# Low weight halves of the first steps on VectorE alone, the first result split behind them; one of the last turned row tiles ahead of the last products, rows sent whole

## The chip, the cores and the metric

The kernel runs on one core of a Trainium2 chip. The time is the device time of one execution in microseconds (us), and the figure used is the median of the runs. Engines are TensorE (PE in the profile, its weight loads PEld), VectorE (DVE), ScalarE (ACT), GpSimd (POOL) and SyncE (SP). An engine's instruction queue bears a small q (SPq).

## The reference

One decoder layer is computed for 512 prompt tokens and for 8 x 4 sample tokens together, 544 rows of width 1024, all in fp32:

```python
def _layer(x, ...):
    m, ... = _mixer(_rmsnorm(x, norm_mix_pre), ...)
    x = x + _rmsnorm(m, norm_mix_post)
    f, ... = _conv_ffn(_rmsnorm(x, norm_ffn_pre), ...)
    return x + _rmsnorm(f, norm_ffn_post)

def _mixer(h, ...):
    xr, q, k, v, g = split(h @ w_in)            # 1024 -> 1024 | 1024 | 256 | 256 | 2048
    lru_out = _rg_lru(_causal_dwconv(xr, ...))
    attn = _band_attention(q, k, v, d, valid, sink, rel_bias)     # window 128, 8 heads on 2
    ...
    merged = sigmoid(g_lru) * (lru_out @ w_lru_o) + sigmoid(g_attn) * (attn @ w_attn_o)
    return merged @ w_out

def _conv_ffn(h, prev, w_up, conv_w, conv_b, w_down):
    u = _causal_dwconv(h @ w_up, ...)           # 1024 -> 8192, width 3
    val, gate = split(u)
    return (gelu(gate) * val) @ w_down          # 4096 -> 1024
```

The scores of the attention get a bias that depends on the distance of query and key, looked up in a table of 32 buckets (`rel_bias`). The states of the recurrences, the last keys and values and the last rows before each convolution are outputs too.

## The kernel before

**How a product is made.** A matrix product in fp32 is three products of split operands: each number is a high half and a low half, and TensorE adds high x high, high x low and low x high into one bank (`mmhalf`). The high half of a weight is a rounded copy by ScalarE (`wsplit_hi`, L275, `wh_in<-raw_in`), and the low half is what is left, raw minus high, by VectorE or GpSimd (`wsplit_lo`, L280, `wl_in<-raw_in,wh_in`). Activations stand turned, features on partitions and tokens along the free side, in two halves of 256 and 288 tokens. `h` is the normalized input, `hH` and `hL` its halves (`hsplit`, L431 and L175).

**The order of the work.** Nearly all instructions stand on their engines in the order in which the program writes them, and semaphores hold an engine until its operands are there. A `step` multiplies one chunk of 128 output columns with one half of the tokens (24 matmuls into a bank `pm...`) and then calls `tick`. A `tick` hands out, in this order: high halves of the next weight units (ScalarE), whatever runs beside (`sides`: the normalization of the second token half, tables, attention), what the step before wanted done with its result (the list `late`), the low halves, and what was put in the list `last`. A weight unit is half a chunk's weights, 128 x 512; a step asks for two of them. Before the change the second low half of a step goes to GpSimd as long as the clock of steps, `now`, is at most 6, and all others go to VectorE.

**The head.** The chunks of the input projection come as two keys and value chunks and the first queries. The first step's bank is `pm_first`; it is filled piece by piece as the turned pieces of `h` come. Its result is a key, whose halves are made by ScalarE (`kH`, L651) and VectorE (`kL`, L166, `kL<-pm_first,kH`). Meanwhile the second token half is normalized: squares of `x` by ScalarE and VectorE (`jv<-x`, L407), the root and its correction (L389, L175), the scaling of the rows (L423), the turning by TensorE (`ps_tb`, L508) and the split into `hH` and `hL`; copies of `x` itself (`xn<-ps_ta`, L483) free the banks that the last turns take. On GpSimd's queue a chain for the bias table runs: `rvec` is written to DRAM (`rscr`), read back spread over the distances (`rrep`, L627) and once more into `btab` (L633). VectorE adds `btab` to the first scores (`s<-psc,btab`, L175); after maxima and the exponential, TensorE turns the weights of the attention (`pt`, L753).

**The tail.** The result of the down projection leaves in rows of tokens. The prompt's first two tiles of 128 tokens are multiplied with tokens on the output's partitions (`ptok`, and for the last 512 columns of tile 1 two pieces of 256, `pend`, made by `ends`), normalized there (`ssq`, the root at L1862, a reciprocal and its correction) and added to `x` (`xtok<-fg,nst_t,xtok`, `tokens_out`), 512 columns at a time. Tiles 2 and 3 and the 32 sample tokens (tile 4) are normalized while still turned (`finish_b`, tiles `ft`), and `rows_t` turns them back: four transposes into a bank `pyo` for each half of 512 columns, a copy by ScalarE into `yo` and a transfer on SP's queue. The function `ends` makes 12 matmuls and two transposing ones for each piece, and both pieces stand ahead of all of `rows_t` on TensorE. The list that sets SP's order at the end is

```python
    yo = [rows_t(i, kk) for i in (2, 3, 4) for kk in range(2)]
    ...
    for f in yo[:3] + xo[:1] + yo[3:4] + xo[1:] + yo[4:]:
        f()
```

Of the kernel before, what the change touches and what calls it, by code (L numbers as in the profile page):

```python
# [17 lines left out]
P = 128  # L18
# [103 lines left out]
def hawk_step(ctx, tc, I, O):  # L122
# [69 lines left out]
    def tick(target=0, dt=1):  # L192
        now[0] += dt
        todo = late[:]
        late.clear()
        split = [wsplit_hi(u) for u in wclaim(target)]
        sides()
        for f in todo:
            f()
        for z, u in enumerate(split):  # L200
            wsplit_lo(*u, eng=pool if z and now[0] <= 6 else None)
        for f in last:
            f()
        last.clear()
# [117 lines left out]
    def step(key, X, a, done, target=None, look=2, quick=False):  # L322

        first_ = key == order[0] and a == 0
        ps = first_ps if first_ else PM("pm" + "_".join(str(z) for z in key) + f"_{a}")
        if first_:
            pass
        elif quick:
            mmhalf(ps, key, X, a, range(4))
            now[0] += 0.5  # L330
            sides()
            mmhalf(ps, key, X, a, range(4, 8))
            done(a, ps)
        else:
            mmhalf(ps, key, X, a)
        tick(upto(key, a, look) if target is None else target, 0.5 if quick else 1)
        if not quick:
            late.append(lambda: done(a, ps))


    xp = I["x_prompt"][0]
# [1385 lines left out]
            if c % 2:  # L1727
                yield 0.5

    def rows_t(i, kk):  # L1730
        t0, nn, _ = TOK[i]
        dst = yp[t0:t0 + nn, :] if i < 4 else ys
        px = PX(f"pyo{i}_{kk}")
        for j in range(4):
            pe.transpose(px[:nn, j * P:(j + 1) * P], ft[4 * kk + j][:, t0:t0 + nn], ident)
        o = S(f"yo{i}_{kk}")[:nn, 0:512]
        act.copy(o, px[:nn, :])
        return lambda: nc.sync.dma_start(out=dst[:, kk * 512:(kk + 1) * 512], in_=o)

    sq7 = T("sq7")  # L1740
    frow, fgs = {}, {}
# [110 lines left out]
    fgs[1, 1] = T("fg1_1")[:, 0:512]  # L1852
    st = SM("nst_t1", [P, 4], "nst_t")
    v, r, s_, b_ = (st[:, z:z + 1] for z in range(4))
    o = ends(0)
    ends_square(0, o)
    ends_gain(0, o)
# [3 lines left out]
    ends_square(1, o)  # L1861
    act.activation(s_, ssq[:, 1, 2:3], AF.Sqrt, scale=1.0 / D, bias=b_)  # L1862
    ends_gain(1, o)
    yo = [rows_t(i, kk) for i in (2, 3, 4) for kk in range(2)]
    stt(v, ssq[:, 1, 2:3], 1.0 / D, b_, ALU.mult, ALU.add)
    dve.reciprocal(r, s_)
    mul(s_, r, r)
    stt(s_, s_, -0.5, v, ALU.mult, ALU.mult)
    stt(r, s_, 1.5, r, ALU.add, ALU.mult)
    xo = [tokens_out(1, r, z) for z in range(2)]  # L1870
    for f in yo[:3] + xo[:1] + yo[3:4] + xo[1:] + yo[4:]:
        f()
    flush()
    order_.close()
# [32 lines left out]
```

## Time and profile before

| | before |
|---|---|
| median of 3 runs, us | 1001.16 (1001.01 to 1002.63) |
| the profiled execution, us | 1000.28 |
| its span, us | 998.3 |
| granted TensorE clock over the span | 0.997 |
| TensorE busy, us | 987.0 |
| VectorE, ScalarE, GpSimd busy, us | 731.4, 580.0, 171.9 |
| moved by DMA | 135.90 MB, mean 136 GB/s |

By stretches of the span, from the busy times of the engines in each:

| stretch, us | length | TensorE busy | VectorE busy | ScalarE busy | GpSimd busy | clock | DMA share |
|---|---|---|---|---|---|---|---|
| 0 to 50 (load, first projections) | 50.0 | 45.97 | 27.87 | 32.05 | 12.82 | 0.97 | 0.70 |
| 50 to 245 | 195.0 | 195.00 | 127.69 | 106.51 | 29.57 | 1.00 | 0.38 |
| 245 to 440 | 195.0 | 195.00 | 124.11 | 107.60 | 68.21 | 1.00 | 0.36 |
| 440 to 600 | 160.0 | 159.61 | 129.98 | 104.13 | 13.45 | 1.00 | 0.57 |
| 600 to 900 | 300.0 | 300.00 | 250.01 | 176.35 | 31.50 | 1.00 | 0.71 |
| 900 to 970 | 70.0 | 69.46 | 55.93 | 45.55 | 6.00 | 1.00 | 0.55 |
| 970 to 998.3 (tail) | 28.3 | 21.98 | 15.81 | 7.78 | 10.31 | 0.95 | 0.22 |

A row of the engines' lists begins with the start time from the span's beginning and the length, both in us, and then has the engine, the line of the program, the operation, what it writes and reads, and the tile's shape. A row that stands for several instructions has their count at its end (x12), and its length reaches from the first's start to the last's end. Square brackets hold the time in which the engine stood idle just before it and what it waited for. The clock is the share of full speed that the chip granted TensorE.

### The profile page before, as it was taken

Reading aid. Unit: us, or ns where it says so; the run is one execution under the profiler, and the core shown is the slowest. Engines: PE = TensorE matmul, PEld = TensorE weight load, DVE = VectorE, ACT = ScalarE, POOL = GpSimd, SP = SyncE. Lnnn points to the kernel's source line nnn. Section 1 sums busy time; section 2 is a strip of 40 time slices with the busy share of each in tenths; the row PEclk is TensorE's granted clock in tenths of the full one; section 3 lists DMA queues with packets and bytes.
Section 4 is the critical chain, followed back from the end, with each engine's and each line's share of the span. In section 5 each row is a group of like instructions: output and inputs, shape, how many; then the busy total and the mean of one; then the engine's idle time right before and its main releaser. Section 6 shows DMA issues by size and latency. Waiting matters only on the chain.

```text
span 998.3 us, 20177 instructions
## 1 busy us (share of the span) xinstructions
PE 987.0 (99%) x7811; PEld 976.8 (98%) x7811; DVE 731.4 (73%) x1533; ACT 580.0 (58%) x1417; POOL 171.9 (17%) x281
## 2 busy tenths in 40 slices
PE   8999999999999999999999999999999999999997
PEld 7999999999999999999999999999999999999996
DVE  6466688545936656589777788888888888888765
ACT  7534455469458625456776656565656565656652
POOL 2252010001404473210001011111110101011004
PEclk9999999999999999999999999999999999999999
DMA  7656323332323635226156767676767676768612
GB/s 209 183 133 214 102 64 106 106 85 81 110 69 100 191 92 144 85 88 206 55 117 140 178 135 184 137 181 140 178 142 175 144 174 147 171 143 206 196 45 90
DMA packets 212118, 135.90 MB, mean 136 GB/s; under 512 B 9549, under 2 KB 197725, under 8 KB 211992
## 3 DMA queue, kind: packets, MB, share of 16 engines
q1 hardware_dynamic: 200056, 113.00, 39.6%
q0 software_dynamic: 11920, 19.59, 12.0%
q10 hardware_dynamic: 48, 2.03, 0.8%
q8 instruction: 61, 1.00, 0.4%
q14 instruction: 33, 0.27, 0.1%
HBM read 112.06 MB, written 11.37 MB: 124 GB/s over the span
## 4 chain that ended last, share of the span: by engine, by line
PE 93%; DVE 2%; ACT 1%; SPq 1%; DMA 1%; issue 0%; ACTq 0%; DVEq 0%
PE pmin L163 21%; PE pmdn L163 17%; PE pux L1458 16%; PE puy L1458 8%; PE pq L1458 6%; PE pmout L163 5%; PE pmao L163 5%; PE pmlo L163 5%; PE puz L1458 4%; PE pg L163 1%; PE psc L163 1%; PE pvp L163 1%; DMA x<-in_x_prompt_dram 1%; SPq L354 1%; PE pt L753 1%; PE ptok L163 1%
## 5 line engine op out<-in xcount | busy, mean ns | idle before, releaser
L163 PE MATMUL pmin<-hH,wh_in 128*128 128x256 f32 (+1 forms) x568 | 166.6, 293 | 0.3 <-ACT wh_in L275 0.3
L163 PE MATMUL pmin<-hH,wl_in 128*128 128x256 f32 (+1 forms) x568 | 164.0, 289 | 1.9 <-DVE wl_in L280 1.9
L163 PE MATMUL pmin<-hL,wh_in 128*128 128x256 f32 (+1 forms) x568 | 164.3, 289 | 0.0
L163 PE MATMUL pmdn<-fH,wh_dn 128*128 128x256 f32 (+1 forms) x448 | 129.4, 289 | 0.2 <-DVE ft L172 0.2
L163 PE MATMUL pmdn<-fH,wl_dn 128*128 128x256 f32 (+1 forms) x448 | 129.0, 288 | 0.0
L163 PE MATMUL pmdn<-fL,wh_dn 128*128 128x256 f32 (+1 forms) x448 | 129.0, 288 | 0.0
L175 DVE SCALAR_TENSOR_TENSOR uc<-u,fv,uc 128x560 f32<-128x560 f32 x128 | 102.1, 798 | 13.3 <-ACT uc L1489 13.2
L163 PEld LDWEIGHTS pmin<-hH,wh_in 128*128 128x128 f32 x568 | 107.9, 190 | 1.9 <-issue 1.2
L163 PEld LDWEIGHTS pmin<-hH,wl_in 128*128 128x128 f32 x568 | 107.6, 189 | 2.1 <-DVE wl_in L280 2.1
L163 PEld LDWEIGHTS pmin<-hL,wh_in 128*128 128x128 f32 x568 | 107.7, 190 | 0.0
L163 PEld LDWEIGHTS pmdn<-fH,wh_dn 128*128 128x128 f32 x448 | 84.4, 188 | 0.6 <-issue 0.6
L163 PEld LDWEIGHTS pmdn<-fH,wl_dn 128*128 128x128 f32 x448 | 84.4, 188 | 0.0
L163 PEld LDWEIGHTS pmdn<-fL,wh_dn 128*128 128x128 f32 x448 | 84.2, 188 | 0.0
L1584 ACT COPY u<-pux 128x272 f32<-128x272 f32 x52 | 20.1, 386 | 84.9 <-PE pux L1458 84.9
L166 DVE TENSOR_TENSOR u<-puy,u 128x240 f32<-128x240 f32 (+2 forms) x78 | 24.7, 344 | 49.3 <-PE puy L1458 32.4
L172 DVE TENSOR_TENSOR ft<-ft,pmdn 128x256 f32<-128x256 f32 (+1 forms) x104 | 45.3, 437 | 17.2 <-PE pmdn L163 16.8
L275 ACT ACTIVATE wh_in<-raw_in 128x512 fp32r<-128x512 f32 x72 | 44.4, 631 | 18.4 <-PE pmin L163 7.1
L1489 ACT ACTIVATE uc<-u,fv 128x560 f32<-128x560 f32 x64 | 48.2, 755 | 0.0
L280 DVE TENSOR_TENSOR wl_in<-raw_in,wh_in 128x512 fp32r<-128x512 f32 x66 | 45.1, 692 | 0.8 <-ACT wh_in L275 0.7
L716 ACT ACTIVATE s<-s,st 128x256 f32<-128x256 f32 (+1 forms) x32 | 15.2, 476 | 48.0 <-DVE st L713 39.6
L1384 POOL DMA_DIRECT2D raw_up_s<-raw_up_s x26 | 22.7, 872 | 100.2 <-DMA raw_up_s<-raw_up__10515 4.5
L166 DVE TENSOR_TENSOR wl_dn<-raw_dn,wh_dn 128x512 fp32r<-128x512 f32 x56 | 38.4, 686 | 0.0
(781 smaller groups left out, 3431.4 us busy)
## 6 DMA issues: line engine op xcount, KB each, us to landing
raw_in<-in_w_in_dram SPq DMA_DIRECT2D x36, 512.0 KB
raw_dn<-in_w_down_dram SPq DMA_DIRECT2D x56, 256.0 KB
raw_up_s<-in_w_up_dram SPq DMA_DIRECT2D x25, 512.0 KB
raw_up_s<-raw_up_s POOLq DMA_DIRECT2D x26, 256.0 KB, 5.9
raw_ao<-in_w_attn_o_dram SPq DMA_DIRECT2D x8, 512.0 KB
raw_lo<-in_w_lru_o_dram SPq DMA_DIRECT2D x8, 512.0 KB
raw_out<-in_w_out_dram SPq DMA_DIRECT2D x8, 512.0 KB
xdram<-xn POOLq DMA_DIRECT2D x8, 272.0 KB, 14.7
```

Of the source, the lines that this page charges most:

```text
L163: pe.matmul(out, l, r, start=start, stop=stop)
L166: dve.tensor_tensor(out=out, in0=a, in1=b, op=ALU.subtract)
L172: dve.tensor_tensor(out=out, in0=a, in1=b, op=ALU.add)
L175: dve.scalar_tensor_tensor(out=out, in0=a, scalar=s_, in1=b, op0=op0, op1=op1)
L275: act.activation(hl[0], raw, AF.Copy)
L280: (eng or dve).tensor_tensor(out=hl[1], in0=raw, in1=f32(hl[0]), op=ALU.subtract)
L354: nc.sync.dma_start(out=xt[i, z][:n, 0:512], in_=src[:, 512 * z:512 * z + 512])
L716: act.activation(s3[:, j, :], s3[:, j, :], AF.Exp, bias=ng[:, j:j + 1], accum_out=sm[:, j:j + 1])
L1384: pool.dma_start(out=w["p4"], in_=w["p2"], accum_op=ALU.add)
L1458: pe.matmul(ps[:, :HN], w, x, start=start and k == 0 and i == 0, stop=stop and k == 3 and i == 2, skip_group_check=True)
L1489: act.activation(yt[j][:, 0:FLATU], u[:, 0:FLATU], AF.Copy, scale=fv[:, j:j + 1])
L1584: act.copy(e[nm_], z)
```

## The change

It has two parts that do not touch each other.

At the head, every low half that a `tick` hands out is made by VectorE, also the second ones of the first ticks that GpSimd made before (the two for the very first step, outside of any tick, stay on GpSimd); and the split of the first step's result (`kH`, `kL`) is put in the list `last` instead of `late`, so that in its tick it comes behind the low halves instead of ahead of them.

At the tail, `rows_t` handles a whole row of 1024 columns: both banks are copied into one tile (from the buffers of the weights, `RAW`), and one transfer takes 1024 columns where two took 512 each. Tile 2 is turned ahead of both pieces of `ends`, tiles 3 and 4 behind them as before. SP's list has the two tiles of prompt rows first, then the first half of the last token-major tile, the sample rows, and its second half.

```diff
--- before.py
+++ after.py
@@ -197,8 +197,8 @@
         sides()
         for f in todo:
             f()
-        for z, u in enumerate(split):
-            wsplit_lo(*u, eng=pool if z and now[0] <= 6 else None)
+        for u in split:
+            wsplit_lo(*u)
         for f in last:
             f()
         last.clear()
@@ -335,7 +335,7 @@
             mmhalf(ps, key, X, a)
         tick(upto(key, a, look) if target is None else target, 0.5 if quick else 1)
         if not quick:
-            late.append(lambda: done(a, ps))
+            (last if first_ else late).append(lambda: done(a, ps))
 
 
     xp = I["x_prompt"][0]
@@ -1727,15 +1727,16 @@
             if c % 2:
                 yield 0.5
 
-    def rows_t(i, kk):
+    def rows_t(i):
         t0, nn, _ = TOK[i]
         dst = yp[t0:t0 + nn, :] if i < 4 else ys
-        px = PX(f"pyo{i}_{kk}")
-        for j in range(4):
-            pe.transpose(px[:nn, j * P:(j + 1) * P], ft[4 * kk + j][:, t0:t0 + nn], ident)
-        o = S(f"yo{i}_{kk}")[:nn, 0:512]
-        act.copy(o, px[:nn, :])
-        return lambda: nc.sync.dma_start(out=dst[:, kk * 512:(kk + 1) * 512], in_=o)
+        o = RAW(f"yo{i}")
+        for kk in range(2):
+            px = PX(f"pyo{i}_{kk}")
+            for j in range(4):
+                pe.transpose(px[:nn, j * P:(j + 1) * P], ft[4 * kk + j][:, t0:t0 + nn], ident)
+            act.copy(o[:nn, kk * 512:(kk + 1) * 512], px[:nn, :])
+        return lambda: nc.sync.dma_start(out=dst, in_=o[:nn, :])
 
     sq7 = T("sq7")
     frow, fgs = {}, {}
@@ -1852,6 +1853,7 @@
     fgs[1, 1] = T("fg1_1")[:, 0:512]
     st = SM("nst_t1", [P, 4], "nst_t")
     v, r, s_, b_ = (st[:, z:z + 1] for z in range(4))
+    yo = [rows_t(2)]
     o = ends(0)
     ends_square(0, o)
     ends_gain(0, o)
@@ -1861,14 +1863,14 @@
     ends_square(1, o)
     act.activation(s_, ssq[:, 1, 2:3], AF.Sqrt, scale=1.0 / D, bias=b_)
     ends_gain(1, o)
-    yo = [rows_t(i, kk) for i in (2, 3, 4) for kk in range(2)]
+    yo += [rows_t(i) for i in (3, 4)]
     stt(v, ssq[:, 1, 2:3], 1.0 / D, b_, ALU.mult, ALU.add)
     dve.reciprocal(r, s_)
     mul(s_, r, r)
     stt(s_, s_, -0.5, v, ALU.mult, ALU.mult)
     stt(r, s_, 1.5, r, ALU.add, ALU.mult)
     xo = [tokens_out(1, r, z) for z in range(2)]
-    for f in yo[:3] + xo[:1] + yo[3:4] + xo[1:] + yo[4:]:
+    for f in yo[:2] + xo[:1] + yo[2:] + xo[1:]:
         f()
     flush()
     order_.close()
```

In the order of VectorE's instructions at the head, seen against the kernel before, each of the first steps gains a second low half, and `kL` moves behind both of its step:

```order
@@ -28,6 +29,7 @@
 L169 TENSOR_TENSOR ss<-ss 128x3
 L175 SCALAR_TENSOR_TENSOR ss<-ss 128x3 x2
-L166 TENSOR_TENSOR kL_396<-pm_first,kH_395 128x256
 L280 TENSOR_TENSOR wl_in_386<-raw_in_125,wh_in_385 128x512
+L280 TENSOR_TENSOR wl_in_389<-raw_in_125,wh_in_388 128x512
+L166 TENSOR_TENSOR kL_398<-pm_first,kH_397 128x256
 L423 TENSOR_SCALAR x_1_115<-x_1_115,ss 128x512
 L423 TENSOR_SCALAR x_1_119<-x_1_119,ss 128x512
@@ -36,4 +38,5 @@
```

The rows `L175 ... ss<-ss` ahead are the end of the root for the second token half, and the rows L423 behind scale its `x`; `kL` stood one row ahead of the low half for the third projection and now stands two rows behind.

On GpSimd the four low halves go, and the chain of the bias table stands alone there:

```order
@@ -13,11 +13,7 @@
 L280 TENSOR_TENSOR wl_in_223<-raw_in_109,wh_in_222 128x512
 L585 MEMSET lt 128x128
-L280 TENSOR_TENSOR wl_in_337<-raw_in_111,wh_in_336 128x512
 L598 MEMSET rvec 8x384
-L280 TENSOR_TENSOR wl_in_389<-raw_in_125,wh_in_388 128x512
 L601 DMA rscr<-rvec 8x384
-L280 TENSOR_TENSOR wl_in_442<-raw_in_134,wh_in_441 128x512
 L627 DMA rrep_324<-rscr 256x1x384
-L280 TENSOR_TENSOR wl_in_501<-raw_in_136,wh_in_500 128x512
 L633 DMA btab_563<-rrep_324 128x2x256
 L627 DMA rrep_325<-rscr 256x1x384
```

Nothing else of GpSimd's order moves; the transfers that stood behind the four subtractions keep their order.

At the end of ScalarE's order, before:

```order
L1782 ACTIVATE jk_0_13517,ssq<-frow_13330 128x512
L1814 ACTIVATE jke_13544,ssq<-pend_13529 128x256
L1814 ACTIVATE jke_13564,ssq<-pend_13549 128x256
L1862 ACTIVATE nst_t_13528<-ssq,nst_t_13528 128x1
L1737 COPY yo_0_13573<-pyo_0_13568 128x512
L1737 COPY yo_1_13580<-pyo_1_13575 128x512
L1737 COPY yo_0_13587<-pyo_0_13582 128x512
L1737 COPY yo_1_13594<-pyo_1_13589 128x512
```

Here `jke<-pend` are the squares of the two last pieces, `nst_t<-ssq` the root, and `yo<-pyo` the copies of turned rows. After:

```order
L1783 ACTIVATE jk_0_13517,ssq<-frow_13330 128x512
L1738 COPY yo_13529<-pyo_0_13530 128x512
L1738 COPY yo_13529<-pyo_1_13536 128x512
L1815 ACTIVATE jke_13557,ssq<-pend_13542 128x256
L1815 ACTIVATE jke_13577,ssq<-pend_13562 128x256
L1864 ACTIVATE nst_t_13528<-ssq,nst_t_13528 128x1
L1738 COPY yo_13581<-pyo_0_13582 128x512
L1738 COPY yo_13581<-pyo_1_13588 128x512
L1738 COPY yo_13594<-pyo_0_13595 32x512
```

The two copies of tile 2 moved ahead of the squares and the root; the four others stay behind it. TensorE's order moved in the same way: the eight transposes of tile 2 stand ahead of the two pieces.

The transfers at the end of SP's order, before:

```order
L1822 DMA out_dram<-xtok_0_13197 128x512
L1822 DMA out_dram<-xtok_1_13237 128x512
L1738 DMA out_dram<-yo_0_13573 128x512
L1738 DMA out_dram<-yo_1_13580 128x512
L1738 DMA out_dram<-yo_0_13587 128x512
L1822 DMA out_dram<-xtok_0_13261 128x512
L1738 DMA out_dram<-yo_1_13594 128x512
L1822 DMA out_dram<-xtok_1_13291 128x512
L1738 DMA out_dram<-yo_0_13601 32x512
L1738 DMA out_dram<-yo_1_13608 32x512
```

And after, with whole rows of 1024 columns:

```order
L1823 DMA out_dram<-xtok_0_13197 128x512
L1823 DMA out_dram<-xtok_1_13237 128x512
L1739 DMA out_dram<-yo_13529 128x1024
L1739 DMA out_dram<-yo_13581 128x1024
L1823 DMA out_dram<-xtok_0_13261 128x512
L1739 DMA out_dram<-yo_13594 32x1024
L1823 DMA out_dram<-xtok_1_13291 128x512
```

Ten issues became seven, tile 2's stands directly behind the first pair of `xtok`, and the last to be issued is now the second half of the last token-major tile instead of the sample rows.

## The prediction

> **What bounds the kernel now.** I read the busy time by stretches first, then the granted clock around the one stretch that is not full, then the engines' rows in it, and last the outflow. In the stretches the columns are length, busy time of TensorE, its weight loads, VectorE, ScalarE, GpSimd, then granted clock, DMA share and GB/s.
>
> ```profile
> span 998.3 us, 20177 instructions
> ...
> PE 987.0 (99%) x7811; PEld 976.8 (98%) x7811; DVE 731.4 (73%) x1533; ACT 580.0 (58%) x1417; POOL 171.9 (17%) x281
> ...
> 0.00:50.00 50.00, 45.97 (x317) 42.26 (x317) 27.87 (x71) 32.05 (x80) 12.82 (x20) 0.97 0.70 196
> ...
> 970.00:998.30 28.30, 21.98 (x152) 19.90 (x151) 15.81 (x43) 7.78 (x22) 10.31 (x11) 0.95 0.22 79
> ...
> 18.99:22.41 3.42, 1.19 (x7) 0.75 (x6) 2.76 (x8) 3.42 (x9) 1.27 (x1) 1.00 0.61 168
> 22.41:25.82 3.41, 3.41 (x18) 3.41 (x17) 1.87 (x5) 3.41 (x10) 1.81 (x2) 0.50 0.19 49
> ...
> 454.00:457.41 3.41, 3.02 (x25) 2.80 (x24) 3.24 (x9) 1.27 (x4) 0.00 (x0) 1.00 0.92 257
> 457.41:460.82 3.41, 3.41 (x28) 3.33 (x27) 2.46 (x10) 0.39 (x1) 0.00 (x0) 1.00 0.89 246
> ```
>
> TensorE is the bound, busy for 987.0 of 998.3 us. Of the 11.3 that it is not, 4.0 lie in the first 50 us and 6.3 after 970, and there this change works. At the head a stretch with 1.19 us of work in 3.42 is followed by one at clock 0.50; a stretch with 3.02 of 3.41 is not.
>
> ```profile
> 21.96 0.38 PE L163 MATMUL pmin<-hH,wl_in 128*128 128x256 f32 x1 [1.91 <-DVE wl_in L280]
> ...
> 26.19 2.18 PE L508 MATMUL ps_tb<-ident,x 128*128 128x128 f32 x12
> 28.30 0.39 PE L163 MATMUL pmin<-hH,wh_in 128*128 128x256 f32 x1
> ...
> 31.25 2.19 PE L508 MATMUL ps_tb<-ident,x 128*128 128x128 f32 x12
> ```
>
> One wait of 1.91 us stands there: the third projection's matmul wants a low half that VectorE (L280) has not made. The 22 matmuls from 21.96 to 26.19 then take 4.23 us; 24 of them between 28.30 and 31.25 take 2.95, so 22 at full clock take 2.70. The wait costs 1.9 and the halved clock after it 1.5.
>
> **The change, head.** Why is the low half late?
>
> ```profile
> 14.74 0.69 DVE L280 TENSOR_TENSOR wl_in<-raw_in,wh_in 128x512 fp32r<-128x512 f32 x1
> 15.35 1.79 DVE L407 SCALAR_TENSOR_TENSOR jv<-x 128x512 f32<-128x512 f32 x1
> ...
> 17.07 0.68 DVE L407 SCALAR_TENSOR_TENSOR jv<-x 128x512 f32<-128x512 f32 x1
> ...
> 19.41 0.36 DVE L175 SCALAR_TENSOR_TENSOR ss<-ss 128x3 f32<-128x3 f32 x2
> 20.31 0.42 DVE L166 TENSOR_TENSOR kL<-pm_first,kH 128x256 fp32r<-128x256 f32 x1 [0.54 <-ACT kH L651]
> 20.65 1.25 DVE L280 TENSOR_TENSOR wl_in<-raw_in,wh_in 128x512 fp32r<-128x512 f32 x1
> ...
> 987.75 1.78 DVE L175 SCALAR_TENSOR_TENSOR xtok<-fg,nst_t,xtok 128x512 f32<-128x512 f32 x1
> ...
> 15.30 1.29 POOL L280 TENSOR_TENSOR wl_in<-raw_in,wh_in 128x512 fp32r<-128x512 f32 x1 [2.17 <-ACT wh_in L275]
> 20.09 1.27 POOL L280 TENSOR_TENSOR wl_in<-raw_in,wh_in 128x512 fp32r<-128x512 f32 x1 [3.15 <-ACT wh_in L275]
> ...
> 987.31 1.67 POOL L1788 TENSOR_TENSOR fg<-frow,gpost 128x512 f32<-128x512 f32 x1 [1.15 <-DVE frow L172]
> ...
> 18.88 1.13 ACT L275 ACTIVATE wh_in<-raw_in 128x512 fp32r<-128x512 f32 x2
> ```
>
> Three VectorE rows are long, and each ends just after a GpSimd row: 17.14 after 16.59, 21.90 after 21.36, 989.53 after 988.98, that is 0.54 to 0.55 each time. VectorE stood until GpSimd was done. The Trainium skill (SBUF — State Buffer, "SBUF: two separate sides") calls the pair of ports that the two share an exclusive lock, held for the whole instruction. The trace agrees, by these three ends. By that rule the sum is the 3.8 us below; were 1.25 us the operation's own length, it would be the second rival's 0.7.
>
> VectorE gains one low half per step, at 0.61 us each (14.74 to 15.35, start to start). In the first step that is +0.61, while the blocked square falls from 1.72 (15.35 to 17.07) to 0.61: -0.5 for all that follows, ScalarE's root and high halves (18.88) with it. In the second step VectorE is free at 19.77 - 0.5 = 19.3, the first high half is there (18.88 + 0.6 - 0.5 = 19.0), and kL no longer stands ahead with its 0.54 of idle time and 0.34 of work. The low half ends at 19.3 + 0.67 = 19.95 instead of 21.90, so TensorE goes on at about 20.0: **1.9 us** earlier. The other low half of the step follows at 20.6, and TensorE wants it at 21.5. The third and fourth step's pairs are +0.6 each, and GpSimd's four rows of 1.3 vanish. kL, 0.5 later, is read only by the scores at 46 us: nothing.
>
> TensorE then has about 2.6 us of work in the 3.4 after 19.0, nearer to the 3.02 that kept the clock than to the 1.19 that lost it. I take the whole **1.5 us**; its bounds are 0 and 1.5. So the transposes at 26.19 start at 22.8, 3.4 earlier. What is late next?
>
> ```profile
> 23.50 1.21 ACT L483 COPY xn<-ps_ta 128x256 f32<-128x256 f32 x4
> ...
> 26.78 2.13 ACT L431 ACTIVATE hH<-ps_tb,pv 128x288 fp32r<-128x288 f32 x4 [0.75 <-PE ps_tb L508]
> ...
> 30.44 0.68 DVE L280 TENSOR_TENSOR wl_in<-raw_in,wh_in 128x512 fp32r<-128x512 f32 x1
> ```
>
> ScalarE. Its copies that free the banks for the last transposes end at 24.71 - 0.5 = 24.2, wanted at 24.4. Its hH then start at 25.5 (the 0.75 of idle time and 0.5 fall away), 1.3 earlier, and VectorE's hL and the fifth projection's first low half with them: done at 31.12 - 1.3 = 29.8, wanted at about 30.2. The second one at 30.4 is wanted at 31.4. Margins of 0.2 to 1.0: thin, but the 3.4 stands; were they overrun, some tenths are lost.
>
> ```profile
> 27.08 1.15 POOL L627 DMA_DIRECT2D rrep<-rscr  x1 [1.03 <-DMA rel<-in_rel_bias_dram]
> 40.60 0.78 POOL L633 DMA_DIRECT2D btab<-rrep  x1 [11.05 <-DMA rrep<-rscr]
> DMA to landing us min/median/max: 4.6/4.6/4.6
> ...
> 46.66 0.42 DVE L175 SCALAR_TENSOR_TENSOR s<-psc,btab 128x256 f32<-128x256 f32 x1 [2.58 <-PE psc L163]
> 52.13 0.48 DVE L724 TENSOR_SCALAR s<-s,st 128x128 f32<-128x128 f32 x2
> ...
> 58.48 0.38 PE L753 MATMUL pt<-ident,s 128*128 128x128 f32 x2
> ```
>
> The bias table becomes a new wait: it lands at 40.60 + 4.6 = 45.2 whatever TensorE does (GpSimd, freed, issues at most 0.7 earlier), and VectorE wants it at 46.66 - 3.4 = 43.3. VectorE stands 1.9 us, with maxima, queries and low halves behind it. TensorE first needs that chain for pt, at 58.48 - 3.4 = 55.1; from the start of s to the last row it needs are 52.61 - 46.66 = 6.0. So s may start as late as 49.1: hidden, 3.9 us to spare.
>
> **The change, tail.**
>
> ```profile
> 989.20 2.78 PE L1735 MATMUL pyo<-ident,ft 128*128 128x128 f32 x24
> ...
> 990.21 0.29 ACT L1862 ACTIVATE nst_t<-ssq,nst_t 128x1 f32<-128x1 f32 x1 [0.25 <-DVE nst_t L1859]
> 990.41 2.94 ACT L1737 COPY yo<-pyo 128x512 f32<-128x512 f32 x6
> ...
> 991.39 1.42 DVE L175 SCALAR_TENSOR_TENSOR xtok<-fg,nst_t,xtok 128x512 f32<-128x512 f32 x2
> ...
> 987.86 2.03 SPq L1822 DMA_DIRECT2D out_dram<-xtok  x2
> 991.00 1.32 SPq L1738 DMA_DIRECT2D out_dram<-yo  x3
> ...
> 991.80:996.60 4.80, 0.18 (x2) 0.00 (x0) 1.00 (x2) 1.55 (x4) 0.00 (x0) 0.85 0.99 355
> ```
>
> The outflow sets the end: from 991.8, 0.8 after the first yo issue, the DMA engines are full (share 0.99) for 4.8 us at 355 GB/s, which is the 1.70 MB of six 256 KB and two 64 KB pieces. In the changed kernel the third token tile (512 KB) leaves right behind the first xtok pair, issued at 989.9, and is gone by 992.3. Its eight transposes (8/24 of 2.78 = 0.93) push both last products back 0.9; the root at 990.21 had about 0.2 of slack, so it moves 0.7. Its two copies sit on ScalarE while that waits for the products: nothing. The fourth tile now needs both its copies (0.49 each, 2.94/6) before its one issue: 990.9 + 0.2 + 1.0 = 992.2, moving from 993.0. Behind it are 1.18 MB, 3.2 to 3.3 us at 355 to 370 GB/s, and the last xtok (992.81 + 0.7 = 993.5) is ready long before its turn: end at 996.2, **0.4 us** earlier. The best case is the last xtok alone, 993.5 + 0.8 + 0.7 = 995.0, a gain of 1.6; the worst is a root later by the full 0.9 and rows of 4 KB no faster to issue, a loss of 0.3. SP has five issues instead of eight, so it is not in the way.
>
> Sum: 1.9 + 1.5 + 0.4 = 3.8 us of the profiled execution's 1000.28 (998.3 and 2.0 around it), so 996.5. The median of the runs shown, 1001.16, lies 0.9 above that execution; the same gain on it gives **997.3 us**. The three runs lie 1.6 us apart, so 0.2% (2 us) is about what can be told from no change.
>
> **Rivals.**
> *The clock pays nothing.* Either TensorE still loses half its clock once, or the timed runs of before did not lose it. The changes of clock at 22.41 and 25.82 are one period apart, and a wait that straddled two periods would show a smaller hole in each. Then 1.9 + 0.4: 998.9. The Trainium skill (TensorE: Matmul & The Clock Gate, "What's actually happening") has such a window: 3413 ns long, free-running, the clock halved after an idle one. The trace agrees on the length (22.41 to 25.82), but lost the clock after a window with 1.19 us of work.
> *The long VectorE rows are their own.* Then the low half takes 1.25 and the squares 1.72 still: VectorE free at 20.4, TensorE on at 21.7, 0.3 gained and the clock lost as before, 0.7 with the tail: 1000.5. Against it stand three equal distances.
> *Slower: the bias table.* If rrep takes over 17.4 us instead of 13.5 (27.08 to 40.60), s starts after 49.1 and TensorE stands one for one; from 21.3 on all 3.8 are gone. Other transfers of this tile did take
>
> ```profile
> DMA to landing us min/median/max: 4.6/11.6/23.9
> ```
>
> and 23.9 would give +2.7: 1003.8. Against it: the weight loads beside this one are issued as before.
>
> **How the numbers follow.** The forecast has 0.72, the clock 0.14, the long rows 0.09, the bias table 0.05. The first's own range is 996.1 (best tail) to 998.2 (no tail, margins overrun by 0.5). The range 995.9 to 999.1 takes in the clock's case and leaves out the last two. Faster by over 0.2% (below 999.2): 0.72 and most of the clock's, 0.83. Within: the rest of it and the long rows, 0.12. Slower: 0.05.
>
> **What would show it.** Right: VectorE's rows at L407 and L280 near 0.68, no TensorE wait above 0.7 us before 30, no clock of 0.50 before the tail, ps_tb from about 22.8, a VectorE wait for btab near 45, out_dram from the third tile near 990, the DMA full only from 993. Wrong: a new wait at ps_tb or for the pairs after 24 us, a halved clock, TensorE waiting at pt, or an outflow that ends no earlier after TensorE's last row than now.

## The result

The changed kernel takes 997.73 us in the median of six runs (997.25 to 998.28), the kernel before 1001.33 in six runs (999.11 to 1002.63). The ratio is 0.9965, with a 95% interval from 0.9953 to 0.9978: faster by 3.6 us, where 997.3 was forecast. The changed kernel's profiled execution took 998.22 us, with a span of 995.9.

First come the head's and the tail's stretches after the change, with the columns of before (length, busy time of TensorE, its weight loads, VectorE, ScalarE, GpSimd, clock, DMA share, GB/s), ahead of them two lines of the page.

```profile
span 995.9 us, 20166 instructions
...
PE 986.5 (99%) x7811; PEld 976.2 (98%) x7811; DVE 731.6 (73%) x1537; ACT 579.7 (58%) x1417; POOL 167.2 (17%) x277
```

```profile
0.00:50.00 50.00, 47.63 (x339) 43.61 (x340) 27.40 (x74) 31.99 (x81) 7.67 (x16) 1.00 0.72 196
...
17.11:20.52 3.41, 3.41 (x28) 2.99 (x27) 3.01 (x13) 2.31 (x8) 0.00 (x0) 1.00 0.99 262
20.52:23.94 3.42, 3.17 (x27) 2.86 (x25) 3.36 (x9) 3.42 (x9) 0.07 (x1) 1.00 0.13 33
```

TensorE works 1.66 us more in the first 50 than before (47.63 beside 45.97) and the clock is full throughout; the period with the wait now holds 3.17 us of its work, where it held 1.19. In the engines' rows at that place:

```profile
16.94 0.69 DVE L407 SCALAR_TENSOR_TENSOR jv<-x 128x512 f32<-128x512 f32 x1
...
20.16 1.29 DVE L280 TENSOR_TENSOR wl_in<-raw_in,wh_in 128x512 fp32r<-128x512 f32 x2
21.38 0.42 DVE L166 TENSOR_TENSOR kL<-pm_first,kH 128x256 fp32r<-128x256 f32 x1
...
20.91 0.39 PE L163 MATMUL pmin<-hH,wl_in 128*128 128x256 f32 x1 [0.25 <-DVE wl_in L280]
23.61 0.82 PE L508 MATMUL ps_tb<-ident,x 128*128 128x128 f32 x4
```

The square that took 1.79 takes 0.69, two low halves together 1.29, kL stands behind them, and TensorE's wait of 1.91 us is one of 0.25. A shorter wait of the kernel before, ahead of the same step, is gone as well; this is its row there:

```profile
19.54 0.39 PE L163 MATMUL pmin<-hH,wh_in 128*128 128x256 f32 x1 [0.32 <-ACT wh_in L275]
```

The transposes at 23.61 stood at 26.19 before, 2.6 earlier; the forecast said 3.4. The difference lies ahead of all that was changed: in this execution the first rows of `x` came later, and the first projection's first matmul (pm_first) starts at 11.78, where it started at 10.79. To compare executions without that, the table cuts each into pieces between three places in TensorE's list: the first matmul of pm_first, the first transpose into ps_tb, the last matmul of ptok, and the end of the span. The head and the middle are differences of two start times in the trace; the end is that of the span, which the page gives to 0.1 us, so the last two columns are good to 0.05.

| kernel | pm_first starts at | to ps_tb (head) | to the last ptok (middle) | to the end (tail) | from pm_first to the end |
|---|---|---|---|---|---|
| before | 10.79 | 15.40 | 959.06 | 13.05 | 987.5 |
| changed | 11.78 | 11.83 | 959.42 | 12.87 | 984.1 |
| e_head | 11.22 | 11.83 | 959.50 | 13.05 | 984.4 |
| e_kl | 10.36 | 12.37 | 958.71 | 13.06 | 984.1 |
| e_lo | 11.46 | 12.79 | 959.06 | 13.09 | 984.9 |
| e_fill12 | 10.79 | 13.91 | 959.29 | 13.11 | 986.3 |
| e_fill4 | 11.96 | 15.41 | 959.03 | 13.10 | 987.5 |
| e_lock | 11.87 | 13.23 | 959.43 | 12.87 | 985.5 |
| e_memset | 11.31 | 11.83 | 959.50 | 12.86 | 984.2 |
| e_late | 10.97 | 11.84 | 959.44 | 13.45 | 984.7 |
| e_half | 12.49 | 11.83 | 959.44 | 12.44 | 983.7 |
| e_mid3 | 10.68 | 11.84 | 959.47 | 12.21 | 983.5 |
| e_halfmid | 13.01 | 12.20 | 959.44 | 12.55 | 984.2 |
| e_klmid | 11.98 | 12.35 | 958.71 | 12.56 | 983.6 |

For the change itself this reads: the head 3.57 us shorter, the tail 0.18 shorter, the middle, which nothing was to touch, 0.36 longer; 3.4 in all. The start of pm_first scatters from 10.36 to 13.01 over these fourteen executions, in no order with what was changed, so a single span says little below 1 us, and the pieces say more. What they leave out is the time outside the span: time less span is 2.36 us in the mean of the changed kernel's six runs and 1.94 in 31 runs of the kernel before, so 0.4 of the 3.4 is given back there.

The new wait that was forecast is there too, and longer:

```profile
40.67 0.78 POOL L633 DMA_DIRECT2D btab<-rrep  x1 [12.43 <-DMA rrep<-rscr]
...
47.21 0.42 DVE L175 SCALAR_TENSOR_TENSOR s<-psc,btab 128x256 f32<-128x256 f32 x1 [5.72 <-DMA btab<-rrep]
...
55.89 0.38 PE L753 MATMUL pt<-ident,s 128*128 128x128 f32 x2
```

VectorE stands 5.72 us, and TensorE does not wait at pt. The last 3.2 of them are for the bias table: TensorE's last product for these scores (psc) ended at 44.03, and for the scores VectorE stood 2.58 us in the kernel before too.

At the tail, the transfers' rows on SP's queue, the root and copies on ScalarE, and stretches of the outflow:

```profile
987.75 2.50 SPq L1739 DMA_DIRECT2D out_dram<-yo  x2
990.66 0.33 SPq L1823 DMA_DIRECT2D out_dram<-xtok  x1
991.09 0.47 SPq L1739 DMA_DIRECT2D out_dram<-yo  x1
991.65 0.55 SPq L1823 DMA_DIRECT2D out_dram<-xtok  x1
...
988.63 0.29 ACT L1864 ACTIVATE nst_t<-ssq,nst_t 128x1 f32<-128x1 f32 x1
988.84 1.99 ACT L1738 COPY yo<-pyo 128x512 f32<-128x512 f32 x4
...
990.55:992.10 1.55, 0.00 (x0) 0.00 (x0) 0.75 (x2) 0.28 (x1) 0.00 (x0) 1.00 0.87 348
992.10:992.75 0.65, 0.00 (x0) 0.00 (x0) 0.00 (x0) 0.00 (x0) 0.00 (x0) 1.00 1.02 362
992.75:993.50 0.75, 0.00 (x0) 0.00 (x0) 0.00 (x0) 0.00 (x0) 0.00 (x0) 0.88 1.13 205
993.50:994.40 0.90, 0.00 (x0) 0.00 (x0) 0.00 (x0) 0.00 (x0) 0.00 (x0) 0.50 0.73 275
```

Tile 2 leaves early, from 987.75 on. What is left runs from 990.55 to 994.40: tile 3, half of the last token-major tile, then from 992.75 on the sample rows in a stretch with 205 GB/s, and last the second half at 275 GB/s, whose issue had ended at 992.20 and whose data waited behind them.

### The profile page after: what moved, and what is told of

Read it like the earlier page. It is cut to its first block, busy times and chain, and to the rows that moved or that the text cites. A ratio compares the mean times of both kernels' runs of the same rounds, so it can differ in the third digit from the quotient of the medians.

```text
span 995.9 us, 20166 instructions
## 1 busy us (share of the span) xinstructions
PE 986.5 (99%) x7811; PEld 976.2 (98%) x7811; DVE 731.6 (73%) x1537; ACT 579.7 (58%) x1417; POOL 167.2 (17%) x277
## 3 DMA queue, kind: packets, MB, share of 16 engines
q0 software_dynamic: 11920, 19.59, 12.1%
## 4 chain that ended last, share of the span: by engine, by line
PE 94%; DVE 2%; DMA 1%; ACT 1%; SPq 1%; issue 0%; DVEq 0%; ACTq 0%
PE pmin L163 21%; PE pmdn L163 17%; PE pux L1458 16%; PE puy L1458 8%; PE pq L1458 6%; PE pmout L163 5%; PE pmlo L163 5%; PE pmao L163 5%; PE puz L1458 4%; PE pg L163 1%; PE psc L163 1%; PE pvp L163 1%; PE ptok L163 1%; SPq L354 1%; DMA raw_in<-in_w_in_dram 1%; PE pt L753 1%
## 5 line engine op out<-in xcount | busy, mean ns | idle before, releaser
L175 DVE SCALAR_TENSOR_TENSOR uc<-u,fv,uc 128x560 f32<-128x560 f32 x128 | 102.0, 797 | 13.3 <-ACT uc L1489 13.2
L172 DVE TENSOR_TENSOR ft<-ft,pmdn 128x256 f32<-128x256 f32 (+1 forms) x104 | 45.2, 435 | 17.1 <-PE pmdn L163 16.5
```

Source lines behind the costliest of these rows:

```text
L172: dve.tensor_tensor(out=out, in0=a, in1=b, op=ALU.add)
L175: dve.scalar_tensor_tensor(out=out, in0=a, scalar=s_, in1=b, op0=op0, op1=op1)
```

## The experiments

**Both halves of the head's change, and each alone.** e_head is the head's change with the tail of before:

```diff
-        for z, u in enumerate(split):
-            wsplit_lo(*u, eng=pool if z and now[0] <= 6 else None)
+        for u in split:
+            wsplit_lo(*u)
...
-            late.append(lambda: done(a, ps))
+            (last if first_ else late).append(lambda: done(a, ps))
```

> The head's two edits alone, with the tail as before. Main theory (the head brings nearly all of the gain): no TensorE wait above 0.4 us between the first projection and 30 us, no granted clock of 0.50 before the tail, 3.4 us less than the kernel before in median (997.9 beside 1001.3). Rival (the tail brings a share of a microsecond or more): under 2.8 us less.

Measured: 998.27 us beside 1000.14 (ratio 0.9980, 0.9971 to 0.9990), 1.9 less. The trace has what was forecast: a head of 11.83, a wait of 0.25, no half clock, and 3.1 us less than the kernel before from pm_first to the end. The timed gain is smaller, and by its number the rival (under 2.8) would have it; but the tail, which the rival wants to bring the rest, brings 0.18 by its own piece. Two figures of the runs make up most of the gap between 3.1 and 1.9. Time less span is 2.33 us in e_head's runs and 1.94 in those of the kernel before. And the profiled execution shows a kernel that loses its clock, which not every run does: of the 31 runs of the kernel before, 20 have a mean granted clock of 0.996 or 0.997 over the span and take 1000.9 us in the mean, 11 have 0.998 or 0.999 and take 999.3; of e_head's ten none is below 0.998. One period of 3.41 us at half the clock is 0.0017 of the span. If those 11 kept their clock, that takes 0.6 from the mean gain (an estimate: 11 of 31 times 1.6). Of the 3.1 are then left 2.1, which is the difference of the means (1000.35 and 998.27).

e_kl changes only the place of kL:

```diff
-            late.append(lambda: done(a, ps))
+            (last if first_ else late).append(lambda: done(a, ps))
```

> Only the first result's split goes behind the low halves; GpSimd still makes every second low half of the first ticks. Theory A (what was late is the low half behind kL, and it can start before GpSimd's subtraction of 20.09): the low half starts at 19.8 in the time of the kernel before, ends near 20.5, TensorE's wait falls from 1.91 to about 0.5 and the clock stays: 2.9 us less than before. Theory B (GpSimd's subtraction blocks it all the same): the low half still ends about 0.55 us behind GpSimd's row, the wait stays above 1.5, the clock is lost: under 0.6 us less.

Measured: 997.12 us (ratio 0.9971, 0.9961 to 0.9980), 3.0 less. GpSimd's, VectorE's and TensorE's rows of this kernel:

```profile
19.67 1.44 POOL L280 TENSOR_TENSOR wl_in<-raw_in,wh_in 128x512 fp32r<-128x512 f32 x1 [3.15 <-ACT wh_in L275]
...
14.91 1.81 DVE L407 SCALAR_TENSOR_TENSOR jv<-x 128x512 f32<-128x512 f32 x1
...
19.27 0.69 DVE L280 TENSOR_TENSOR wl_in<-raw_in,wh_in 128x512 fp32r<-128x512 f32 x1
...
20.23 1.16 DVE L423 TENSOR_SCALAR x<-x,ss 128x512 f32<-128x512 f32 x1
...
20.02 0.39 PE L163 MATMUL pmin<-hH,wl_in 128*128 128x256 f32 x1 [0.39 <-DVE wl_in L280]
```

Theory A, within about a tenth. The low half starts at 19.27, ahead of GpSimd's subtraction, and takes its 0.69; the subtraction still stretches the square (1.81) and now a scaling of `x` (1.16), and neither is waited for. GpSimd's own row, which began 0.40 us after the low half, takes 1.44 where it took 1.27. One moved line brings 3.0 of the head's 3.57 us.

e_lo is the other half alone:

```diff
-        for z, u in enumerate(split):
-            wsplit_lo(*u, eng=pool if z and now[0] <= 6 else None)
+        for u in split:
+            wsplit_lo(*u)
```

> Only the low halves move to VectorE; kL stays ahead of them. Theory A (GpSimd's subtractions were what stretched VectorE's rows): the squares and low halves take 0.70 us each, the low half that TensorE waits for starts 0.9 us later than in the changed kernel, TensorE's wait is about 1.1 us, and with some 2.3 us of work in the 3.4 us window the clock stays: 2.5 us less than before. Rival (a wait of 1.1 us already costs the clock): 1.0 us less, with a stretch at 0.50. Rival (kL's place is what counts): no gain.

Measured: 998.54 us (ratio 0.9984, 0.9974 to 0.9993), 1.6 less; by the pieces 2.6 less from pm_first on, all of it in the head. TensorE's row, and the period with the wait:

```profile
21.54 0.39 PE L163 MATMUL pmin<-hH,wl_in 128*128 128x256 f32 x1 [1.22 <-DVE wl_in L280]
...
17.88:21.29 3.41, 2.44 (x19) 1.89 (x17) 2.47 (x12) 2.46 (x6) 0.00 (x0) 1.00 0.82 224
```

The wait is 1.22 where 1.1 was expected, and a period with 2.44 us of work keeps the clock. The hole lay across the end of that period, with 0.97 us of it inside; still, none of the ten timed runs has a clock below 0.998. The two halves of the head's change are not additive: 3.0 and 2.6 alone, 3.6 together, since either alone saves the clock's 1.5, and the wait of 1.9 can be saved only once.

**Is the halved clock a cost of its own?** e_fill12 keeps everything of the kernel before and makes TensorE work through its wait:

```diff
         else:
+            if key == order[2] and a == 0:
+                for _ in range(12):
+                    mm(ps[:, :256], wunits[2 * wpos[key]][0][:, 0, :], X.get(0, a, 0), True, True)
             mmhalf(ps, key, X, a)
```

> The kernel before with one matmul of the third projection made twelve more times ahead of its wait (1.4 us of TensorE work, overwritten by the thirteenth), nothing else changed. Theory A (the halved clock follows from the hole in TensorE's work, and is a cost of its own): the low half still ends at the same time, TensorE's wait falls to about 0.5, no stretch at 0.50 follows, and the kernel takes 1.5 us less than before. Rival (the clock falls for another reason, or the timed runs did not lose it): no gain, or the stretch at 0.50 is still there.

```profile
19.55 1.80 PE L163 MATMUL pmin<-hH,wh_in 128*128 128x256 f32 x13 [0.31 <-ACT wh_in L275]
21.99 0.38 PE L163 MATMUL pmin<-hH,wl_in 128*128 128x256 f32 x1 [0.53 <-DVE wl_in L280]
...
20.13:23.55 3.42, 2.89 (x25) 2.69 (x24) 3.24 (x7) 3.42 (x10) 1.26 (x1) 1.00 0.24 68
23.55:26.96 3.41, 3.41 (x25) 2.57 (x24) 1.26 (x4) 3.41 (x11) 2.03 (x2) 1.00 0.17 31
```

The low half comes at the same time, 21.99, and still the head is 1.49 us shorter (13.91 beside 15.40): in the profiled execution the halved clock is a separate 1.5. In time the kernel is at 999.89 beside 1000.14 (ratio 0.9993, 0.9983 to 1.0004), which shows no 1.5. The clocks given above account for a part: where the kernel before kept its clock there was nothing to gain, so the fill could bring about 1.0 in the mean (1000.35 less 999.3). It brought 0.55 (999.80), with one of its ten runs at a clock of 0.997. Why a part of the runs would keep the clock is argued and not shown: the periods run on at a phase of their own, and a hole of 1.9 us that falls across two of them leaves each with more work. The traces show the phase: within each, all changes of the clock lie whole multiples of 3.41 us apart, and the first period at full clock begins anywhere from 4.35 to 7.64 us in the fourteen. A trace of the kernel before with its hole across two periods is not among them.

e_fill4 puts four matmuls in place of twelve:

```diff
-                for _ in range(12):
+                for _ in range(4):
```

> The kernel before with four repeated matmuls (0.5 us) ahead of the wait, where the run with twelve kept the clock. TensorE then has about 1.7 us of work in the period of 3.41 us with the hole, between the 1.18 that lost the clock and the 2.44 that kept it. If half a period of work is needed: lost or kept by a hair; wait near 1.4. If the clock is lost only when the work falls to about a third: no stretch at 0.50, TensorE 1.5 us earlier from 26 us on. If the hole lies across two periods, both hold more work and the clock stays in any case.

```profile
20.08:23.50 3.42, 1.66 (x12) 1.17 (x12) 2.68 (x8) 3.42 (x10) 1.27 (x1) 1.00 0.17 42
23.50:26.91 3.41, 3.41 (x19) 3.41 (x18) 1.96 (x5) 3.41 (x10) 1.72 (x2) 0.50 0.15 31
```

With 1.66 us of work in the period the clock is lost, and the head is as long as before (15.41). So far, then: lost at 1.19 and 1.66, kept at 2.44, 2.89 and 3.17. The Trainium skill (TensorE: Matmul & The Clock Gate, "What's actually happening") speaks of an idle window of 3413 ns; the length agrees with these periods, but a period that was half full was enough here.

**Does GpSimd's subtraction hold VectorE up?** e_lock is the changed kernel with the four subtractions back on GpSimd, into a tile that nobody reads:

```diff
+    scr = cp.tile([P, 4, P], F32R, name="scr")
...
-        for u in split:
+        for z, u in enumerate(split):
+            if z and now[0] <= 6:
+                pool.tensor_tensor(out=scr, in0=u[0], in1=f32(u[1][0]), op=ALU.subtract)
             wsplit_lo(*u)
```

> The changed kernel with the four subtractions put back on GpSimd as well, into a tile that nobody reads (GpSimd's work as before, VectorE's as after, no new wait between them). Theory A (a GpSimd subtraction holds VectorE up while it runs): in the first two ticks one VectorE row each of 1.7 to 2.0 us that ends 0.55 us behind GpSimd's row; TensorE's wait for the third projection's first low half grows from 0.25 to 0.8 to 1.5 us or a second wait appears at its second low half; 0.5 to 1.5 us slower than the changed kernel, 1.5 more if the clock goes. Rival (the long rows came from elsewhere): every row stays at 0.70 and the time at the changed kernel's 997.7.

```profile
16.38 1.29 POOL L204 TENSOR_TENSOR scr<-raw_in,wh_in 128x512 fp32r<-128x512 f32 x1 [2.18 <-ACT wh_in L279]
21.82 1.38 POOL L204 TENSOR_TENSOR scr<-raw_in,wh_in 128x512 fp32r<-128x512 f32 x1 [3.80 <-issue]
...
16.43 1.79 DVE L284 TENSOR_TENSOR wl_in<-raw_in,wh_in 128x512 fp32r<-128x512 f32 x1
...
21.98 1.78 DVE L284 TENSOR_TENSOR wl_in<-raw_in,wh_in 128x512 fp32r<-128x512 f32 x1
...
21.22 0.38 PE L163 MATMUL pmin<-hH,wh_in 128*128 128x256 f32 x1 [0.92 <-ACT wh_in L279]
22.12 0.39 PE L163 MATMUL pmin<-hH,wl_in 128*128 128x256 f32 x1 [0.39 <-DVE wl_in L284]
```

Two low halves that took 0.69 take 1.79 and 1.78, and each ends 0.55 to 0.56 us after GpSimd's row (18.22 after 17.67, 23.76 after 23.20). The tile is read by nobody, so no data joins the two engines there. The head grows by 1.40; the time is 999.57 beside 1000.82 (ratio 0.9991, 0.9979 to 1.0003), 1.2 more than e_memset below has beside the same runs. So the rows were long because of GpSimd, not by themselves. The wait moved: not the low half but the high half is late most (0.92), since the first stretched row pushes the squares, the root (at 20.36 on ScalarE, 8.49 after pm_first; 7.37 in the changed kernel) and with it ScalarE's next high halves.

e_memset has GpSimd write only:

```diff
-                pool.tensor_tensor(out=scr, in0=u[0], in1=f32(u[1][0]), op=ALU.subtract)
+                pool.memset(scr, 0.0)
```

> As the one above, but GpSimd only writes: a memset of 128x512 in place of each subtraction. If any GpSimd instruction holds VectorE up: one long VectorE row per tick as there, longer by the memset's length. If only one that reads SBUF does: VectorE's rows stay at 0.70, TensorE's wait at 0.25, the time at the changed kernel's 997.7.

```profile
13.59 0.53 POOL L204 MEMSET scr<- 128x512 f32 x1
14.42 0.52 POOL L204 MEMSET scr<- 128x512 f32 x1
```

Head 11.83, time 998.34 (ratio 0.9975, 0.9965 to 0.9986): as the changed kernel. But this run doesn't answer its question. A memset waits for nothing, so the first two ran at 13.59 and 14.42, ahead of the low halves at 15.26, and met none of VectorE's rows with two operands from SBUF (the on-chip memory that both engines read and write). The third, at 24.13, began inside a low half that had started first and kept its 0.69. Whether a GpSimd instruction that only writes holds VectorE up stays open.

**The tail: the early tile or the whole rows?** e_late turns tile 2 behind the last products again:

```diff
-    yo = [rows_t(2)]
     o = ends(0)
...
-    yo += [rows_t(i) for i in (3, 4)]
+    yo = [rows_t(i) for i in (2, 3, 4)]
```

> The changed kernel with whole-row transfers, but tile 2 turned behind both last products again. From the last token-major matmul (ptok) to the end of the span the kernel before takes 13.05 us in every tail like it, the changed kernel 12.87. If the early tile brings the gain: 13.0 to 13.2, since the first whole row of a tile is ready 0.5 us later than its half was. If the whole rows bring it: 12.9 or less.

The tail is 13.45 us, 0.4 longer than before: worse than either expectation. e_half has the early tile with half rows:

```diff
-    def rows_t(i):
+    def rows_t(i, kk):
...
-        o = RAW(f"yo{i}")
-        for kk in range(2):
...
+        o = S(f"yo{i}_{kk}")[:nn, 0:512]
+        act.copy(o, px[:nn, :])
+        return lambda: nc.sync.dma_start(out=dst[:, kk * 512:(kk + 1) * 512], in_=o)
...
-    yo = [rows_t(2)]
+    yo = [rows_t(2, kk) for kk in range(2)]
...
-    for f in yo[:2] + xo[:1] + yo[2:] + xo[1:]:
+    for f in yo[:4] + xo[:1] + yo[4:] + xo[1:]:
```

> The changed kernel with tile 2 turned early as there, but transfers of half rows as before. The run without the early tile lost 0.58 us of tail against the changed kernel (13.45 from the last ptok to the end of the span, beside 12.87) and 0.4 against the kernel before (13.05), so whole rows should cost 0.4 and the early tile bring 0.6: 12.4 to 12.5. Rival (whole rows pay here, since fewer issues stand in SP's queue): 12.9 or more.

12.44, as expected. So the early tile brings 0.6 (13.05 to 12.44, and 13.45 to 12.87) and the whole rows cost 0.4 (13.05 to 13.45, and 12.44 to 12.87); the change's 0.18 is what is left of the two. The rows of SP's queue, of e_late and then of e_half:

```profile
988.47 1.31 SPq L1739 DMA_DIRECT2D out_dram<-yo  x2
989.87 0.41 SPq L1823 DMA_DIRECT2D out_dram<-xtok  x1
990.37 1.03 SPq L1739 DMA_DIRECT2D out_dram<-yo  x1
991.49 0.55 SPq L1823 DMA_DIRECT2D out_dram<-xtok  x1
```

```profile
988.44 2.55 SPq L1738 DMA_DIRECT2D out_dram<-yo  x4
991.39 0.33 SPq L1822 DMA_DIRECT2D out_dram<-xtok  x1
991.81 0.88 SPq L1738 DMA_DIRECT2D out_dram<-yo  x2
992.78 0.38 SPq L1822 DMA_DIRECT2D out_dram<-xtok  x1
```

The last ptok of e_late starts at 982.25, so its first whole row is issued 6.22 us after it, where the first half row of before went 5.75 after it (991.00 less 985.25). Its one issue of the sample rows takes 1.03 us, and the last piece stands behind that issue. In e_half the two issues of the sample rows take 0.88 together, and tile 3's first half is issued 6.39 us after ptok, where its whole row in the changed kernel waits for the second copy until 6.88.

Half rows have a price too, which is paid behind the data. The last stretch of the span, in which the DMA engines move nothing more, is 1.70 us before and 1.40 in the changed kernel; here is that stretch, first of before, then of the changed kernel:

```profile
996.60:998.30 1.70, 0.00 (x0) 0.00 (x0) 0.00 (x0) 0.00 (x0) 0.00 (x0) 0.50 0.00 0
```

```profile
994.50:995.90 1.40, 0.00 (x0) 0.00 (x0) 0.00 (x0) 0.00 (x0) 0.00 (x0) 0.50 0.00 0
```

By the packets in the trace, the data end at 996.63 and 994.59, and the stretch behind them is 1.69 and 1.36 us. It is 1.67 to 1.69 in all nine kernels with half rows and 1.35 to 1.37 in the five with whole rows; why is not shown. So the data of the changed kernel end 11.56 us after the last ptok, 0.18 later than before (11.38), and what the tail gains it gains behind the data. Counted to the last packet, the early tile brings 0.6 (e_late's 12.13 to 11.56, and 11.38 to e_half's 10.75), and the whole rows cost 0.8, of which they give 0.3 back behind the data.

e_mid3 turns tile 3 between the two last products and sends the sample rows ahead of the last pair:

```diff
+    yo += [rows_t(3)]
     o = ends(1)
...
-    yo += [rows_t(i) for i in (3, 4)]
+    yo += [rows_t(4)]
...
-    for f in yo[:2] + xo[:1] + yo[2:] + xo[1:]:
+    for f in yo + xo:
```

> The changed kernel with tile 3 turned between the two last products as well, and the sample rows sent ahead of the last token-major pair. If the outflow still sets the end, its second half starts 1.7 us earlier, the end is set by the last products' chain (0.9 later): 12.4 from the last ptok to the end of the span, beside 12.87. If the chain of the last products is what sets the end already: 13.5 or more.

12.21, the shortest tail of all, and 996.54 us in its one run. Which of its two moves brings it was not run apart. e_halfmid does the same with half rows:

```diff
-    yo += [rows_t(3)]
+    yo += [rows_t(3, kk) for kk in range(2)]
     o = ends(1)
...
-    yo += [rows_t(4)]
+    yo += [rows_t(4, kk) for kk in range(2)]
```

> Both: half rows, tiles 2 and 3 ahead of the last product's second piece. From the last ptok to the end 12.1 (0.8 less than the changed kernel); time 0.8 less than the changed kernel, 3.9 to 4.4 less than the kernel before. If SP's issues (0.45 each, twelve of them) set the end: 12.5 or more.

Here the forecast of 12.1 missed: 12.55. Once tiles 2 and 3 leave early, whole rows are better than half rows by 0.3. The last pair is issued at the same distance from ptok in both (8.5 and 9.2 us after it), and the last packet ends 10.9 us after ptok in both. So the 0.3 lies in the stretch behind the data, which is 1.67 here, with ten transfers at the end, and 1.37 in e_mid3, with seven. In time it takes 997.87 us beside 1001.70 (ratio 0.9963, 0.9951 to 0.9976). Its profiled execution was a late starter, with a clock of its own to tell of:

```profile
7.77:11.18 3.41, 1.40 (x11) 1.02 (x10) 2.86 (x11) 1.47 (x3) 0.00 (x0) 1.00 1.06 327
11.18:14.59 3.41, 3.41 (x18) 3.41 (x17) 1.72 (x5) 2.26 (x6) 2.25 (x2) 0.50 1.08 293
```

The rows of `x` came so late that TensorE stood 1.94 us before them, and the period with 1.40 us of work cost the clock once more, here at a cost of about 0.4 in the head (12.20).

e_klmid is that tail with only kL moved at the head:

```diff
+    yo = [rows_t(2, kk) for kk in range(2)]
     o = ends(0)
...
-            late.append(lambda: done(a, ps))
+            (last if first_ else late).append(lambda: done(a, ps))
```

> The tail of the run above, and at the head only kL behind the low halves, GpSimd keeping its second halves. If GpSimd's removal adds nothing that can be measured once kL has moved (the runs of either head were 997.1 with GpSimd and 998.3 without, with the same tail): the same time as the run above within 0.5 us, or up to 1 us faster. If the 0.4 us that the trace shows in favour of VectorE alone counts: 0.4 slower.

997.85 us (ratio 0.9959, 0.9946 to 0.9973), the same as e_halfmid. Its head is 0.5 longer than with VectorE alone and its middle 0.7 shorter. So by this pair moving kL is all of the head's change that the time shows. e_kl and e_head, a pair with the tail of before and ten runs each beside the same runs, go further: e_kl, in which GpSimd keeps its subtractions, is the faster by 1.15 us (996.58 to 998.00 beside 997.74 to 998.88). Of that 0.2 to 0.3 are in the pieces and 0.4 outside the span (1.96 beside 2.33); the rest stays open. No run shows a gain in time from taking the subtractions off GpSimd once kL has moved. None of these is faster than the changed kernel beyond the scatter of the runs: by the pieces e_mid3 and e_klmid are 0.6 and 0.5 shorter than it, and e_mid3 was run once.

## Why the prediction was right

The direction came as forecast, and the two large terms as worked out for the profiled execution. That the time came within 0.4 us is in part luck: the same head brought 1.9 in e_head's runs and, with the changed kernel's tail, 2.5 in e_memset's, and terms that the prediction did not have pull both ways.

- **The wait, 1.9.** From pm_first to the matmul that waits, the changed kernel takes 9.13 us (20.91 less 11.78), before 11.17 (21.96 less 10.79): 2.04 less. It is made up otherwise than forecast: 0.25 of the wait is left, and a wait of 0.32 for the high half just ahead of it, of which the prediction did not speak, is gone; the rest is the matmuls between. The low half ended 9.08 after pm_first, the prediction's 19.95 is 9.16.
- **VectorE held up by GpSimd.** The equal distances of 0.54 to 0.55 meant what they were taken for. e_lock shows it directly (0.69 became 1.79 and 1.78). The Trainium skill's exclusive lock (SBUF — State Buffer, "SBUF: two separate sides") agrees, and its word that the one that starts first has the ports for the whole instruction is what e_kl lives on: there the low half, begun first, keeps its 0.69.
- **The clock, 1.5.** The rest of the head's 3.57 is 1.53, and e_fill12 alone has 1.49. The step took the full 1.5 for the timed runs as well, and neither e_fill12's time nor the clocks of the runs bear that out: with 20 of 31 runs that lose it, the term is about 1.0 in the mean (an estimate: 20 of 31 times 1.6). So the rival that the timed runs of before did not lose their clock holds for about a third of them.
- **The margins behind.** None was overrun: behind its wait at 20.91 the changed kernel's TensorE stands again only at 452.89 (0.42 us), where it stands in the kernel before too (0.39).
- **The bias table.** The step had the right wait and the right cover, and the wrong size. The table held VectorE for 3.2 us, not 1.9: `s` started at 47.21 where 45.2 was worked out for the table, because the 4.6 us from issue to landing became 6.4, while TensorE was only about 0.8 later than in the prediction's time. `pt` starts at 55.89 and the chain from `s` to it takes 6.0 as before (47.21 to 53.16), so 2.7 us were left of the 3.9.
- **The tail, 0.4.** It was 0.18, and not in the way that was worked out. The fourth tile is issued 6.88 us after the last ptok, 992.1 in the prediction's time, where it had 992.2. Mis-sized is the step "Behind them are 1.18 MB, 3.2 to 3.3 us at 355 to 370 GB/s": the outflow took 3.85 (990.55 to 994.40), since the stretch with the sample rows went at 205 GB/s and the last one at 275. The data so end 0.18 later behind ptok, not 0.4 earlier, and 4.83 us behind TensorE's last row (989.76) where it was 4.65 (991.98): an outflow that ends no earlier, which the prediction had named as a sign of being wrong. What made it a gain is the stretch behind the data, 0.33 shorter, which the prediction did not have. The Trainium skill (SBUF — State Buffer, "Door 1: The DMA port swizzle (why `[64,N]` ≈ `[32,N]`)") gives 32 partitions 8 of 16 ports and about 218 GB/s; the 205 of that stretch are near it, and the rule was there to be used. The two parts of the tail's change were not weighed apart: the early tile gained 0.6, and the whole rows, of which the sum had only the wait for a second copy, lost 0.4.
- **What was counted at nothing.** The 959 us between head and tail grew by 0.36, and the 2.0 us outside the span by 0.4.

The sum by the pieces is 3.57 + 0.18 - 0.36 = 3.4, and 3.0 less what was lost outside the span; the forecast is 3.8, the medians' difference 3.6.

## What to carry to other kernels

When an operation of one engine is long in only some of its rows, compare its end with the ends of the other engines' rows: an equal distance each time names the holder, and moving the one operation that is waited for ahead of the holder's start can bring nearly as much as taking the holder away (3.0 of the head's 3.6 us here, by one line, and in the timed runs no less than the whole). Count a hole in TensorE's work with the clock that may follow it, and don't expect that in every execution. Of a tail that the outflow sets, send early what is ready early (0.6 us here); making transfers larger paid only where none of them had to wait for its second half. Keeping transfers from few partitions away from the end looks right by one stretch at 205 GB/s, but was not run by itself. Look at the end of the data and at the end of the program apart.

## What was not expected of the hardware

- The middle of the program, which no kernel here changes, takes 958.71 us in both kernels that only move kL, 959.03 to 959.06 in three kernels with kL in its old place, and 959.42 to 959.50 in the eight in which kL is moved and VectorE makes all low halves; only e_fill12 stands between, with 959.29. Kernels with the same head differ by less than 0.1 there, so this is not the scatter of single executions. The difference builds up in small steps, forward and back, over hundreds of matmuls, without a wait. The cause stays open.
- The first projection starts between 10.36 and 13.01 us, with the rows of `x` that come late, in kernels whose load is issued alike.
- Time less span is 1.86 to 2.02 us in the mean of the runs of seven kernels (before, e_kl, e_lo, e_fill12, e_fill4, e_lock, e_klmid) and 2.29 to 2.36 in the seven others. Each of the others has both halves of the head's change. Of the seven only e_lock has both, and GpSimd subtracts there. The cause stays open.
- Behind the last packet of data the program takes another 1.67 to 1.69 us with half rows and 1.35 to 1.37 with whole rows.
- A period with 1.66 us of TensorE work in 3.42 lost half the clock for the next one; one with 2.44 didn't.
